# A hybrid encoder layer on one core: fp16 high and low parts for the dense products of its four passes, with scales from bounds that the chip computes

## The chip, the cores and the metric

The kernel runs on one core of one Trainium2 chip. The time is the device time of one execution in microseconds (us), and the figure for a kernel is the median of its runs. Before the change it is 2885.89 us (three runs, 2879.7 to 2888.39). The engines are called as in the profile: PE is TensorE, with PEld for its weight loads, DVE is VectorE, ACT is ScalarE, POOL is GpSimd, and SP is SyncE, whose queue issues the transfers (DMA).

## What is computed

One encoder layer on x of 2048 tokens by 1024 features and a memory of 256 tokens, all in float32. From the reference, cut to what matters:

```python
y = rmsnorm(h, norm_mix_g) @ w_in            # q, k, v (512 each), conv a and g (512 each)
att  = dilated_sliding_attention(q, k, v)     # three windows: (128,1), (512,4), (2048,16)
conv = conformer_conv(a, g, conv_w, conv_b, conv_ln_g, conv_ln_b)
h = h + concatenate([att, conv]) @ w_out      # 1024 x 1024
xq = rmsnorm(h, norm_x_g) @ w_xq              # 4 heads of 256
mn = rmsnorm(mem, norm_mem_g); xk, xv = mn @ w_xk, mn @ w_xv
pr = softmax(einsum('bshd,bmhd->bhsm', xq, xk) * 256 ** -0.5)
h = h + einsum('bhsm,bmhd->bshd', pr, xv) @ w_xo
u = rmsnorm(h, norm_mlp_g) @ w_up             # 1024 x 4096
h = h + square(relu(u)) @ w_down              # 4096 x 1024
return rmsnorm(h, norm_final_g)
```

## The kernel before

The matrices are worked in tiles of 128 by 128 weights against 512 columns (tokens). To keep float32's accuracy, each factor is split into a high and a low part, and each product is three matmuls, high by high, high by low and low by high (`mm3`, L248 to L252; the three matmuls are the lines L250, L251 and L252 of the profile).

The work has these stages, in order of time:

- **Memory, to about 140 us** (`memory`, L404). The memory's keys are folded with w_xq into the scratch array `ascr`, its values with w_xo into `bscr`. So cross attention becomes two dense products, with `ascr` (called xs) and with `bscr` (called x). Beside it `xprep` (L378) normalises x, turns it and splits it; the squares of its rows go through a tile "junk" (L366).
- **The w_in products, about 140 to 440 us.** Units `glu` (L566, tiles g00, a00, g10, a10), `lin_qk` (L670, tiles kr, qr, k0, q0, k1, q1, k2, q2) and `lin_v` (L623) run through `pipeline` (L550), which starts a unit's load, its scale and its split some steps ahead of its matmuls. Here the split is already fp16: `wscale` (L183) squares a raw weight tile on ACT with a sum (L189), and `pow2` (L168) makes a power of two from it by a small PE product (tile p, L173), a POOL power and DVE steps; `wsplit16` (L203) scales the tile (L207), casts its high part to fp16 on ACT and takes the low part on POOL. Parts of the convolution's sums (tile cacc, L267, on DVE) are woven in.
- **Far attention, to about 755 us**, with the rest of the `glu` units woven in. Outputs of attention and convolution go as high and low parts into the scratch arrays `cath` and `catl`.
- **Four passes of 512 tokens** (`post(p)`, L1310), from about 755 us to the end. Each does the product with w_out (called o), the product with ascr (xs), a softmax (tile xp), the product with bscr (x), then eight groups of w_up (up) and w_down (dn). The last pass has its own form of the MLP (`last_mlp`, L1459), where w_down is applied with seven products in place of eight on sums of halves.

In the passes each weight tile of 512 KB goes through `wpost` (L1179). SP loads it into one of two buffers "raw"; `wsplit2` makes the parts:

```python
    def wsplit2(wp, raw, name, bufs=2, shape=(P, 8, P), lo_eng=None):
        hi = wp.tile(list(shape), F32R, tag="whi", name=f"whi_{name}", bufs=bufs)
        lo = wp.tile(list(shape), F32R, tag="wlo", name=f"wlo_{name}", bufs=bufs)
        ACT.copy(hi, raw)                                               # L240
        (lo_eng or DVE).tensor_tensor(lo, raw, f(hi), op=ALU.subtract)  # L241
```

F32R is the form of float32 that PE takes at one pass. The split tiles alternate between two pools of two, so four are alive. A finished product is added to the residual stream h on DVE (L1303 for o and x, L1430 for dn, L1571 in the last MLP), and h is split again with a gain (L1304 on ACT, L1305 on DVE).

While pass p runs, two side streams are woven between its steps: the near attention of pass p+1 and its convolution. `weave` (L93) sets how many of their steps go with one step of the main stream. The order of the program is written by hand this way; a scheduler then orders each engine's queue by estimated times. Each engine takes its queue in order, and so does SP: a load that waits for its buffer holds back all loads behind it.

Of the kernel before, what the change touches and what calls it, by code (L numbers as in the profile page):

```python
# [48 lines left out]
def hybrid_layer(ctx, tc, A, out):  # L49
# [67 lines left out]
    cath = [dr.tile([P, S], F32R, name=f"cath{k}") for k in range(KC)]  # L117
    catl = [dr.tile([P, S], F32R, name=f"catl{k}") for k in range(KC)]
# [19 lines left out]
    cst.tile([P, 56], F32, name="cpad")  # L138
# [8 lines left out]
    def setup():  # L147
# [15 lines left out]
        sq = lp.tile([P, 8], F32, tag="nsq", name="gsq")  # L163
        ACT.activation(sq, gv[:, 0:8], AF.Square, accum_out=sx[:, 3:4])
        pow2(sx[:, 0:1], sx[:, 1:2], sx[:, 3:4], 1024.0)
        DVE.tensor_scalar(gmix, gv[:, 0:8], sx[:, 0:1], None, op0=ALU.mult)

    def pow2(mul, inv, ss, target, *names):  # L168

        with ExitStack() as st:  # L170
            after(st, *names)
            pc = ps("c", "p2")
            PE.matmul(pc[:, 0:1], onesq, ss, start=True, stop=True)  # L173
            v = lp.tile([P, 4], F32, tag="p2", name="p2", bufs=2)
            DVE.tensor_scalar(v[:, 0:1], pc[:, 0:1], 1e-30, None, op0=ALU.max)
            POOL.tensor_tensor(v[:, 1:2], v[:, 0:1], mhalf, op=ALU.pow)
            DVE.tensor_scalar(v[:, 2:3], v[:, 1:2], target, None, op0=ALU.mult)
            DVE.tensor_scalar(mul.bitcast(I32), v[:, 2:3].bitcast(I32), 0x7F800000, None, op0=ALU.bitwise_and)
            DVE.reciprocal(inv, mul)
# [3 lines left out]
    def wscale(raw, key):  # L183

        if key in tiles_scaled:
            return
        n = tiles_scaled[key] = 4 * len(tiles_scaled)
        q = lp.tile([P, 1024], BF16, tag="wjunk", name="wjunk")
        ACT.activation(q, raw.rearrange("p a b -> p (a b)"), AF.Square, accum_out=wsc[:, n + 3:n + 4])  # L189
        pow2(wsc[:, n:n + 1], wsc[:, n + 1:n + 2], wsc[:, n + 3:n + 4], 32768.0, "pe", "dve")  # L190
        t = wsc[:, n + 1:n + 2]
        DVE.tensor_tensor(t, t, sx[:, 1:2], op=ALU.mult)
        if key[0] == "a":
            c = cw[:, key[1]]
            DVE.tensor_scalar(c, c, t, None, op0=ALU.mult)
        else:
            DVE.tensor_scalar(wsc[:, n + 2:n + 3], t, 0.5 if key[0] == "g" else -0.125, None, op0=ALU.mult)
# [39 lines left out]
    def wsplit2(wp, raw, name, bufs=2, shape=(P, 8, P), lo_eng=None):  # L237
        hi = wp.tile(list(shape), F32R, tag="whi", name=f"whi_{name}", bufs=bufs)
        lo = wp.tile(list(shape), F32R, tag="wlo", name=f"wlo_{name}", bufs=bufs)
        ACT.copy(hi, raw)  # L240
        (lo_eng or DVE).tensor_tensor(lo, raw, f(hi), op=ALU.subtract)  # L241
# [31 lines left out]
    def conv_ln(n, alloc):  # L273
# [45 lines left out]
        for c in range(4):  # L319
            th_ = alloc("hi", F32R, f"lh{n}_{c}")  # L320
            tl_ = alloc("lo", F32R, f"ll{n}_{c}")
            ACT.copy(th_, cs[c])
            POOL.tensor_tensor(tl_, cs[c], f(th_), op=ALU.subtract)
            dma(f(cath[4 + c][:, sl]), f(th_))
            dma(f(catl[4 + c][:, sl]), f(tl_))
# [5 lines left out]
    xna = {n: pool(f"x{n}", stack=lin) for n in (2, 3)}  # L331
    lp = pool("lin", stack=lin)
    onesq = lp.tile([P, P], F32, name="onesq")
    DVE.memset(onesq, 1.0)
    gmix = lp.tile([P, 8], F32, name="gmix")
    sx = lp.tile([P, 4], F32, name="sx")
    wsc = lp.tile([P, 96], F32, name="wsc")
    lp.tile([P, 248], F32, name="lpad")
    xna.update({n: pool(f"x{n}", stack=early, side="right") for n in (0, 1)})
    XH_ = {}  # L340
# [5 lines left out]
    def xtiles(n):  # L346
        for i in range(KC // 2):
            for part, dst in (("h", XH_), ("l", XL_)):
                t = xpool(part, i, n, f"x{part}{i}_{n}", dtype=F16)
                dst[2 * i, n], dst[2 * i + 1, n] = t[:, 0], t[:, 1]  # L350
# [17 lines left out]
    def rstd_nat(sp, nat, name):  # L368
# [5 lines left out]
        DVE.tensor_tensor(ss[:, 0:n], ss[:, 0:n], ss[:, n:2 * n], op=ALU.add)  # L374
        rstd_col(r[:, 0:n], ss[:, 0:n], n, sp)
# [28 lines left out]
    def memory(sp):  # L404
# [76 lines left out]
        for h in range(XH):  # L481
            wt, wts = wts, []
            for k2 in range(4):
# [8 lines left out]
                DVE.tensor_tensor(ev, pt, rbm.rearrange("p q m -> p (q m)"), op=ALU.mult)  # L492
                dma(ascr[h // 2, :, 2 * k2:2 * k2 + 2, 256 * (h % 2):256 * (h % 2) + 256],
# [14 lines left out]
        for h in range(XH):  # L508
            wt, wts = wts, []
            for mc in range(2):  # L510
                for nh in range(2):
# [8 lines left out]
                    ACT.activation(ev, pt, AF.Copy, scale=rmem[:, mc:mc + 1])  # L520
                    dma(bscr[4 * nh:4 * nh + 4, :, 2 * h + mc, :].rearrange("m p c -> p m c"),
# [28 lines left out]
    def pipeline(*units):  # L550

        for _ in range(3):
            next(units[0])
        for _ in range(2 if len(units) > 1 else 0):
            next(units[1])
        for i, u in enumerate(units):
            if i + 1 < len(units):
                next(units[i + 1])
            if i + 2 < len(units):
                next(units[i + 2])  # L560
            for j, _ in enumerate(u):
                if j == 0 and i + 2 < len(units):
                    next(units[i + 2])
                yield

    def glu(c, ns, fine=False):  # L566
# [4 lines left out]
        def unit(x, c0):  # L571
# [3 lines left out]
            wscale(raw, (x, c))  # L575
# [47 lines left out]
    def lin_v(g, ns):  # L623
# [6 lines left out]
        yield  # L630
        wh = lbv.tile([P, 8, 256], F16, tag="wvh", name=f"wvh{g}{ns[0]}")
# [38 lines left out]
    def lin_qk(isq, c):  # L670
# [6 lines left out]
        if c == "r":  # L677
# [4 lines left out]
            wscale(raw, key)  # L682
# [5 lines left out]
        else:  # L688
# [3 lines left out]
            wscale(raw, key)  # L692
# [108 lines left out]
    with ExitStack() as st:  # L801
# [16 lines left out]
        drain(later)  # L818
    edges()
    vsc = vscale()  # L820
    with ExitStack() as st:
# [3 lines left out]
        weave(islice(steps, 31), (vsc, 0.42), (conv0, 0.58))  # L825
        drain(vsc, conv0)
        next(steps)
    with ExitStack() as st:
# [3 lines left out]
        for _ in range(4):  # L832
            next(steps)
        weave(islice(steps, 8), (conv0, 1))
        for _ in range(4):
            next(steps)
        weave(steps, (conv0, 2.2))
        drain(conv0)
# [136 lines left out]
    def combine(p, pr, o0):  # L975
# [46 lines left out]
        ct = [cats[0][x, pr] if end else aq.tile([P, 512], F32R, tag=f"ct{x}", name=f"ct{x}{p}{pr}") for x in "hl"]  # L1022
        with ExitStack() as st:
# [4 lines left out]
            vs = vinv[:, pr:pr + 1]  # L1028
            ACT.activation(ct[0], pt, AF.Copy, scale=vs)
            DVE.scalar_tensor_tensor(ct[1], pt, vs, f(ct[0]), op0=ALU.mult, op1=ALU.subtract)  # L1030
        for t, d in () if end else zip(ct, (cath, catl)):
            dma(f(d[pr][:, 512 * p:512 * (p + 1)]), f(t))
# [146 lines left out]
    def wpost(src, name, shape=(P, 8, P)):  # L1179
# [5 lines left out]
        return wsplit2(wq if n % 4 > 1 else wp, raw, name, shape=shape)  # L1185
# [3 lines left out]
    def ahead(m):  # L1189
# [4 lines left out]
        wout[m] = wsplit2(wp, raw, f"o0{m}")  # L1194
# [48 lines left out]
    def xquad(q, j, name):  # L1243
        return xp_.tile([P, 4, 512], F32R, tag=f"x{q}{j}", name=name)

    def ytile(q, k, name, dtype=F32R):
# [33 lines left out]
    def load_pair(p, half, j):  # L1280
        for q, src in (("h", cath), ("l", catl)):
            for e in range(1 if p == 0 and half and j else 2):
                k = 4 * (1 - half) + 2 * j + e
                dma(f(cats[p][q, k]), f(src[k][:, 512 * p:512 * (p + 1)]))

    def resid_linear(load, rhs, korder, resid, hs, ssum, key, y, name, steps=False, wide=False):


        for ms in ((0, 1, 2, 3) if wide else (0, 1, 2), () if wide else (3,), (4,), (5,), (6,), (7,)):
# [3 lines left out]
            for ks in [korder[a:b] for a, b in zip(cuts, cuts[1:])] if len(ms) > 1 else (korder,):  # L1293
                for m, (wh, wl) in zip(ms, wt):
# [6 lines left out]
                    if ks[-1] == korder[-1]:  # L1301
                        h = hs[m]
                        last["dve"] = DVE.tensor_tensor(h, pts[m], resid(m), op=ALU.add)  # L1303
                        ACT.activation(y["h", m], h, AF.Copy, scale=gain(key, m))  # L1304
                        DVE.scalar_tensor_tensor(y["l", m], h, gain(key, m), f(y["h", m]), op0=ALU.mult,  # L1305
                                                 op1=ALU.subtract)
# [3 lines left out]
    def post(p):  # L1310
# [9 lines left out]
        def from_x(m):  # L1320
# [6 lines left out]
        yield from resid_linear(lambda m: wout[m] if p == 0 and m in wout else wpost(wcols(w_out, m * P), f"o{p}{m}"),  # L1327
                                cats[p], [4, 5, 6, 7, 0, 1, 2, 3], from_x, hs, ssum, "x", y, f"o{p}_",
                                p == 0, p == 0)
        rs = rstd_from(ssum)  # L1330
# [356 lines left out]
```

## Time and profile before

| | before |
|---|---|
| median of the runs | 2885.89 us |
| the profiled execution | 2877.99 us, its span 2876.2 us |
| mean granted clock of PE | 0.988 |
| PE busy | 2783.7 us, 97% of the span |
| DVE busy | 1979.6 us, 69% |
| ACT busy | 1250.5 us, 43% |
| POOL busy | 467.2 us, 16% |
| moved by DMA | 434.27 MB, mean 151 GB/s |

The shares are means over stages that differ. A busy PE is not a PE at its peak, since a matmul's time in the records overlaps that of the next; the interval between the starts of two matmuls tells the rate.

### The profile page before, as it was taken

The page shows a single profiled execution, that of the slowest core. Times are in us where ns is not written, and L with a number is a line of the kernel's source. Part 1 is how long each engine was busy: PE and PEld are TensorE (multiplying, and loading weights), DVE is VectorE, ACT ScalarE, POOL GpSimd, SP SyncE. Part 2 cuts the span into 40 slices and gives each one's busy share as a digit, 9 for nine tenths or more (in the row PEclk, how much of TensorE's full clock was granted, in tenths as well). Part 3 has the DMA queues.
Part 4 walks back from the last instruction along what each step waited for, and adds up shares of the span by engine and source line. Part 5 has one row for each costly group of instructions (what it writes and reads, how often), then busy time and mean ns, then how long its engine had stood idle before and what let it go on. Part 6 is the DMA issues. An engine that isn't in the chain of part 4 may idle for free.

```text
span 2876.2 us, 41437 instructions
## 1 busy us (share of the span) xinstructions
PE 2783.7 (97%) x15474; PEld 2211.0 (77%) x15474; DVE 1979.6 (69%) x3579; ACT 1250.5 (43%) x2089; POOL 467.2 (16%) x500
## 2 busy tenths in 40 slices
PE   7889999988899999999999999999999999999998
PEld 7844467667688888888888888888888888888887
DVE  5636645555589886556887865579887556569886
ACT  5644332365454333434543334345433434444443
POOL 1236531121201111210020112001120110000000
PEclk9999999999999999999999999999999999999999
DMA  9968864789744544555444545544444445223342
GB/s 265 291 150 215 209 171 109 182 229 249 196 124 127 139 128 125 161 150 176 117 126 130 138 126 163 163 137 127 132 129 139 133 158 181 87 85 99 92 117 66
DMA packets 590729, 434.27 MB, mean 151 GB/s; under 512 B 191581, under 2 KB 508433, under 8 KB 590016
## 3 DMA queue, kind: packets, MB, share of 16 engines
q1 hardware_dynamic: 549776, 407.68, 50.4%
q10 hardware_dynamic: 38528, 17.93, 2.4%
q0 software_dynamic: 2224, 6.01, 0.6%
q8 instruction: 122, 2.00, 0.3%
q14 instruction: 79, 0.65, 0.1%
HBM read 340.42 MB, written 91.11 MB: 150 GB/s over the span
## 4 chain that ended last, share of the span: by engine, by line
PE 59%; DVE 5%; DMA 2%; ACT 1%; issue 1%; POOL 1%; SPq 0%; ACTq 0%; POOLq 0%; DVEq 0%
PE dn L250 7%; PE dn L252 7%; PE dn L251 7%; PE up L250 7%; PE up L252 7%; PE up L251 7%; DVE cacc L267 2%; PE o L251 2%; PE o L250 2%; PE o L252 2%; PE xs L250 2%; PE xs L252 2%; PE xs L251 1%; PE s L1082 1%; DMA cath<-lh 1%; PE pt L860 1%
## 5 line engine op out<-in xcount | busy, mean ns | idle before, releaser
L250 PE MATMUL up<-mh,whi_u 128*128 128x512 f32 x1024 | 403.4, 394 | 0.0
L251 PE MATMUL up<-ml,whi_u 128*128 128x512 f32 x1024 | 399.6, 390 | 2.4 <-DVE ml L1305 2.4
L252 PE MATMUL up<-mh,wlo_u 128*128 128x512 f32 x1024 | 399.2, 390 | 0.0
L267 DVE SCALAR_TENSOR_TENSOR cacc<-cu,cw,cacc 128x512 f32<-128x512 f32 x480 | 384.7, 802 | 5.1
L250 PE MATMUL dn<-hhh,whi_d 128*128 128x512 f32 x768 | 299.1, 399 | 1.1 <-ACT hhh L1416 1.1
L251 PE MATMUL dn<-hhl,whi_d 128*128 128x512 f32 x768 | 298.6, 391 | 0.6 <-DVE hhl L1417 0.6
L252 PE MATMUL dn<-hhh,wlo_d 128*128 128x512 f32 x768 | 298.2, 391 | 0.0
L240 ACT CAST whi_u<-raw_u 128x1024 fp32r<-128x1024 f32 x128 | 134.6, 1051 | 262.6 <-PE dn L251 187.9
L240 ACT CAST whi_d<-raw_d 128x1024 fp32r<-128x1024 f32 x100 | 105.1, 1051 | 317.1 <-PE up L251 270.9
L251 PEld LDWEIGHTS up<-ml,whi_u 128*128 128x128 f32 x1024 | 192.5, 188 | 41.2 <-DVE ml L1305 3.7
L252 PEld LDWEIGHTS up<-mh,wlo_u 128*128 128x128 f32 x1024 | 192.2, 188 | 40.5
L250 PEld LDWEIGHTS up<-mh,whi_u 128*128 128x128 f32 x1024 | 192.4, 188 | 37.3
L241 DVE TENSOR_TENSOR wlo_u<-raw_u,whi_u 128x1024 fp32r<-128x1024 f32 x128 | 160.8, 1257 | 45.7 <-ACT whi_u L240 40.5
L1430 DVE TENSOR_TENSOR h<-h,dn 128x512 f32<-128x512 f32 x192 | 128.5, 683 | 84.0 <-PE dn L252 83.1
L1414 DVE SCALAR_TENSOR_TENSOR rl<-up,ssumx 128x512 f32<-128x512 f32 x96 | 66.0, 690 | 167.3 <-PE up L252 166.5
L853 DVE CUSTOM_DVE_ANT_0 sm<-s,mask 128x256 f32<-128x256 f32 (+1 forms) x384 | 127.9, 374 | 69.5 <-PE s L1082 47.3
L252 PEld LDWEIGHTS dn<-hhh,wlo_d 128*128 128x128 f32 x768 | 144.1, 188 | 30.7
L250 PEld LDWEIGHTS dn<-hhh,whi_d 128*128 128x128 f32 x768 | 143.7, 188 | 29.7 <-ACT hhh L1416 1.3
L251 PEld LDWEIGHTS dn<-hhl,whi_d 128*128 128x128 f32 x768 | 144.6, 188 | 28.3 <-DVE hhl L1417 1.5
L864 DVE TENSOR_TENSOR pl<-pt,ph 128x512 f16<-128x512 f32 x160 | 109.8, 687 | 54.6 <-ACT ph L863 53.9
L227 POOL TENSOR_TENSOR nr<-st_v,mhalf 128x4 f32<-128x4 f32 (+1 forms) x15 | 14.3, 950 | 817.3 <-DVE st_v L223 817.3
L854 ACT ACTIVATE sm<-sm,o 128x256 f32<-128x256 f32 (+1 forms) x288 | 116.9, 454 | 59.4 <-DVE o L853 58.5
(497 smaller groups left out, 6945.9 us busy)
## 6 DMA issues: line engine op xcount, KB each, us to landing
raw_u<-in_w_up_dram SPq DMA_DIRECT2D x128, 512.0 KB
raw_d<-in_w_down_dram SPq DMA_DIRECT2D x100, 512.0 KB
raw_o<-in_w_out_dram SPq DMA_DIRECT2D x32, 512.0 KB
raw_a<-ascr SPq DMA_DIRECT2D x32, 512.0 KB
raw_b<-bscr SPq DMA_DIRECT2D x32, 512.0 KB
b<-in_w_down_dram SPq DMA_DIRECT2D x28, 512.0 KB
k<-kscr SPq DMA_DIRECT2D x24, 512.0 KB
k<-kscr SPq DMA_DIRECT2D x8, 1152.0 KB
```

The source lines that it names most:

```text
L240: ACT.copy(hi, raw)
L241: (lo_eng or DVE).tensor_tensor(lo, raw, f(hi), op=ALU.subtract)
L250: PE.matmul(o, lh, rh, start=first, stop=False, skip_group_check=more)
L251: PE.matmul(o, lh, rl, start=False, stop=False, skip_group_check=more)
L252: last["pe"] = PE.matmul(o, ll, rh, start=False, stop=end, skip_group_check=more)
L267: DVE.scalar_tensor_tensor(acc, u[:, t:t + 512], cw[:, c, t:t + 1], acc, op0=ALU.mult, op1=ALU.add)
L853: last["dve"] = DVE.tensor_tensor_reduce(dst, so, mask[:, 256 * m:256 * m + nk], 1.0, 3e38, ALU.add, ALU.min, mn)
L854: last["act"] = ACT.activation(dst, dst, AF.Exp, bias=mn, scale=-1.0)
L860: last["pe"] = PE.transpose(pt[:, j, :], sm[:, j, :], ident)
L864: DVE.tensor_tensor(pl, pt, ph, op=ALU.subtract)
L1414: last["dve"] = DVE.scalar_tensor_tensor(r, pt, 0.0, rsb, op0=ALU.max, op1=ALU.mult)
L1430: last["dve"] = DVE.tensor_tensor(hs[m], hs[m], pt, op=ALU.add)
```

## The change

**fp16 in the passes.** High and low parts of weights and activations of the five dense products become fp16 in place of F32R, and so do `cath` and `catl`, with half the bytes. fp16 has a small range, so every factor gets a power of two as scale, and the product is scaled back where it is used:

```diff
-        ACT.copy(hi, raw)
-        (lo_eng or DVE).tensor_tensor(lo, raw, f(hi), op=ALU.subtract)
+        ACT.activation(hi, raw, AF.Copy, scale=scale)
+        DVE.scalar_tensor_tensor(lo, raw, scale, hi, op0=ALU.mult, op1=ALU.subtract)
```

```diff
-                        last["dve"] = DVE.tensor_tensor(h, pts[m], resid(m), op=ALU.add)
-                        ACT.activation(y["h", m], h, AF.Copy, scale=gain(key, m))
+                        g = gains[:, m:m + 1]
+                        last["dve"] = DVE.scalar_tensor_tensor(h, pts[m], scale, resid(m), op0=ALU.mult, op1=ALU.add)
+                        ACT.activation(y["h", m], h, AF.Copy, scale=g)
...
-                    last["dve"] = DVE.tensor_tensor(hs[m], hs[m], pt, op=ALU.add)
+                    last["dve"] = DVE.scalar_tensor_tensor(hs[m], pt, K_DN, hs[m], op0=ALU.mult, op1=ALU.add)
```

The adds of `last_mlp` change in the same way. `conv_ln` gets one more POOL product per tile (16 in all), for the scale of its output.

**The scales.** They come from the sums of squares of the weights, so every weight has to be seen before its first use. New generators load the weights a first time and square them on ACT:

```diff
+    def scan(sc):
+        def one(src, shape, i):
+            t = sc.tile([P, 1024], F32, tag="scan", name=f"scan{i}", bufs=3)
+            q = sc.tile([P, 1024], BF16, tag="sjunk", name=f"sjunk{i}")
+            dma(t.rearrange("p (a b) -> p a b", a=shape), src)
+            yield
+            ACT.activation(q, t, AF.Square, accum_out=acc2[:, i:i + 1])
+        gens = [one(wcols(w_up, P * i), 8, i) for i in range(32)]
+        gens += [one(wcols(w_out, 0, 1024, rows=(i, i + 1)), 1, 32 + i) for i in range(8)]
+        yield from loads_ahead(gens)
...
+    def scan_down(sc):
+        def one(i):
+            t = sc.tile([P, 1024], F32, tag="scan", name=f"scand{i}", bufs=2)
+            q = sc.tile([P, 1024], BF16, tag="sjunk", name=f"sjunkd{i}")
+            dma(t, w_down[P * i:P * i + P, :])
+            yield
+            ACT.activation(q, t, AF.Square, accum_out=acc2[:, 76 + i:77 + i])
+        yield from loads_ahead([one(i) for i in range(32)])
...
+        pow2(S_DN, I_DN, None, 16384.0, "dve", of=t)
```

`loads_ahead` issues the load of a tile one step before the square of the one ahead of it. `scan` has 40 tiles of 512 KB, `scan_down` 32. In `memory`, each of the 32 tiles that go to `ascr` and `bscr` gets a square as well, through the tile "junk":

```diff
+                q_ = sp.tile([P, 512], BF16, tag="junk", name="junk", bufs=1)
+                ACT.activation(q_, ev, AF.Square, accum_out=acc2[:, 36 + 4 * h + k2 + 4:37 + 4 * h + k2 + 4])
```

`bounds` follows `scan`: one PE product that sums over the partitions, some 40 DVE operations on single columns, and four calls of `pow2` for the scales of weights and activations.

**Where this stands.** The scans are woven into the w_in products and into the first nine steps of pass 0:

```diff
+    scn = chain(scan(scp), bounds())
...
-        weave(islice(steps, 31), (vsc, 0.42), (conv0, 0.58))
+        weave(islice(steps, 31), (vsc, 0.42), (conv0, 0.58), (scn, 0.4))
...
-        weave(steps, (conv0, 2.2))
-        drain(conv0)
+        weave(islice(steps, 4), (scn, 1))
+        weave(islice(steps, 8), (conv0, 1), (scn, 1))
+        weave(islice(steps, 4), (scn, 1))
+        weave(steps, (conv0, 2.2), (scn, 2))
+        drain(conv0, scn)
...
+            dsc = scan_down(pp)
...
+        if p == 0:
+            weave(islice(main, 9), (dsc, 4), *sides)
+            drain(dsc)
```

**w_in's scales a step later.** `wscale` now yields between the square and `pow2`, and `pipeline` starts its first two units one step further ahead:

```diff
         ACT.activation(q, raw.rearrange("p a b -> p (a b)"), AF.Square, accum_out=wsc[:, n + 3:n + 4])
+        yield
         pow2(wsc[:, n:n + 1], wsc[:, n + 1:n + 2], wsc[:, n + 3:n + 4], 32768.0, "pe", "dve")
...
-        for _ in range(3):
+        for _ in range(4):
             next(units[0])
-        for _ in range(2 if len(units) > 1 else 0):
+        for _ in range(3 if len(units) > 1 else 0):
             next(units[1])
```

Some small constants move to another pool, and the tiles of x for token groups 2 and 3 are laid out anew, so that the scan's buffers find room where group 2's pool lay.

258 lines of the change are left out of this document (185 added, 73 removed).

## The prediction

> **What bounds the kernel now.** The first view is the page's table of engines: TensorE (PE) is busy for nearly the whole span and no other engine for more than 69%. I read next the windows view, because a mean over 2.9 ms says nothing about a stage.
>
> ```profile
> span 2876.2 us, 41437 instructions
> PE 2783.7 (97%) x15474; PEld 2211.0 (77%) x15474; DVE 1979.6 (69%) x3579; ACT 1250.5 (43%) x2089; POOL 467.2 (16%) x500
> DVE  5636645555589886556887865579887556569886
> ```
>
> ```profile
> 70.00:110.00 40.00, 37.24 (x316) 36.99 (x315) 33.98 (x54) 25.08 (x47) 13.31 (x10) 1.00 1.05 332
> 140.00:200.00 60.00, 51.17 (x244) 25.63 (x245) 24.64 (x57) 31.65 (x47) 21.64 (x18) 0.94 0.53 125
> 180.00:190.00 10.00, 7.69 (x33) 3.74 (x32) 2.89 (x9) 6.58 (x11) 3.32 (x3) 0.83 0.66 175
> 200.00:260.00 60.00, 53.70 (x256) 25.85 (x254) 30.75 (x48) 31.91 (x41) 36.33 (x35) 0.94 0.84 217
> 260.00:330.00 70.00, 65.88 (x304) 30.12 (x303) 54.22 (x81) 25.67 (x33) 41.37 (x40) 0.98 0.94 214
> 735.00:755.00 20.00, 9.13 (x49) 6.69 (x50) 3.20 (x11) 2.49 (x7) 1.44 (x2) 0.66 0.94 258
> 755.00:865.00 110.00, 107.61 (x607) 89.41 (x607) 88.82 (x180) 54.47 (x104) 12.55 (x14) 1.00 0.49 137
> 864.00:936.00 72.00, 71.13 (x411) 58.74 (x410) 66.64 (x121) 36.23 (x60) 11.96 (x13) 1.00 0.45 126
> ```
>
> The columns are the window, then busy us of PE, weight loads, VectorE (DVE), ScalarE (ACT) and GpSimd (POOL), the granted clock, the DMA share and GB/s. Three regimes stand there. From 755 us on, in the four passes, PE is the bound, but in the densest window DVE has 66.6 of 72 us filled. From 140 to 330 us, where the w_in products run, PE has 19 us of idle time in 190 and the DMA engines are already at 0.53, 0.84 and 0.94. Around 735–755 PE waits for transfers, and its granted clock is 0.66. The change makes the first regime's instructions shorter, and puts its extra work into the second and into the beginning of the first.
>
> **The gain on PE.** The groups of instructions give the counts, the timeline the interval between two matmuls that follow each other (a single one's duration overlaps its neighbours).
>
> ```profile
> L250 PE MATMUL up<-mh,whi_u 128*128 128x512 f32 x1024 | 403.4, 394 | 0.0
> L250 PE MATMUL dn<-hhh,whi_d 128*128 128x512 f32 x768 | 299.1, 399 | 1.1 <-ACT hhh L1416 1.1
> L250 PE MATMUL o<-cath,whi_o 128*128 128x512 f32 x256 | 102.5, 402 | 2.1 <-DMA cath<-cath 1.4 <-ACT cath L1029 0.7
> L250 PE MATMUL xs<-whi_a,yh 128*128 128x512 f32 x256 | 101.4, 398 | 0.0
> L250 PE MATMUL x<-pth,whi_b 128*128 128x512 f32 x256 | 100.7, 399 | 0.7 <-ACT pth L1357 0.7
> L250 PE MATMUL dn<-whi_d,hqh 128*128 128x512 f32 x112 | 43.7, 390 | 0.5 <-ACT hqh L1482 0.5
> L250 PE MATMUL dn<-whi_d,hz 128*128 128x512 f32 x84 | 32.7, 389 | 0.0
> L250 PE MATMUL dn<-whi_d,hhh 128*128 128x512 f32 x32 | 12.3, 389 | 0.0
> ```
>
> ```profile
> 2000.00 0.39 PE L252 MATMUL x<-pth,wlo_b 128*128 128x512 f32 x1
> ...
> 2002.72 0.39 PE L252 MATMUL x<-pth,wlo_b 128*128 128x512 f32 x1
> ```
>
> ```profile
> 299.54 0.38 PE L251 MATMUL lin<-xl,whi_k 128*128 128x512 f16 x1
> ...
> 302.99 0.38 PE L252 MATMUL lin<-xh,wlo_k 128*128 128x512 f16 x1
> ```
>
> Each group has two equal partners, L251 and L252, so the matmuls that change are 3 x (1024 + 768 + 256 + 256 + 256 + 112 + 84 + 32) = 8364. In the fp32r run 12 intervals take 2.72 us, 226.7 ns each; in the fp16 run of the w_in products, which is the same three-product form, 16 take 3.45 us, 215.6 ns. That is 11.1 ns x 8364 = 92.8 us. PE is the bound there, so it is a gain: **-93**.
>
> **What DVE and ACT pay.** The residual adds and the lower halves of the weights become scaled operations.
>
> ```profile
> L241 DVE TENSOR_TENSOR wlo_u<-raw_u,whi_u 128x1024 fp32r<-128x1024 f32 x128 | 160.8, 1257 | 45.7 <-ACT whi_u L240 40.5 <-DMA catl<-ll 4.9
> L1430 DVE TENSOR_TENSOR h<-h,dn 128x512 f32<-128x512 f32 x192 | 128.5, 683 | 84.0 <-PE dn L252 83.1
> L1305 DVE SCALAR_TENSOR_TENSOR yl<-h,gv,yh 128x512 fp32r<-128x512 f32 x32 | 23.4, 747 | 0.0
> L240 ACT CAST whi_u<-raw_u 128x1024 fp32r<-128x1024 f32 x128 | 134.6, 1051 | 262.6 <-PE dn L251 187.9 <-DMA raw_u<-in_w_up_dram 31.1 <-PE dn L252 17.5
> L207 ACT ACTIVATE raw_a<-raw_a,wsc 128x1024 f32<-128x1024 f32 x8 | 9.2, 1145 | 23.6 <-DMA raw_a<-in_w_in_dram 20.9 <-DVE wsc L178 2.7
> ```
>
> An operation on two tensors with a column scalar takes 747 ns, the plain one 683: +64 ns. By the program's loops there are 88 weight tiles and 80 residual adds in each of three passes and 109 and 122 in the last: 735 x 64 ns = 47 us of DVE over the 2010 us from 865 to the end; if the extra doubles with the 1024-wide tile, 71 us. ACT's scaled copy takes 1145 against 1051 ns, 373 x 94 ns = 35 us, on an engine that has half of its time free (36 of 72 us in the dense window): nothing. For DVE, the 72 us of the dense window shrink to 68.6 us on PE (5% of it, 11.1/226.7) while DVE's 66.6 grow by its share of 47 us, 72 x 47/2010 = 1.7, to 68.3 us. [...] The page's row of DVE has three slices of 40 at 9 tenths and ten at 8; each slice is 72 us and would gain 3.4. I let the three lose all of it, and the ten about a tenth of a slice's gain: 10 + 4, **+14**, with ends 5 and 44 (all thirteen slices gain nothing).
>
> **The scans in the w_in stage.** Forty new loads of 512 KB, each squared by ACT, go before the end of the w_in products; their results are needed by the first split of w_out, which is much later, so nothing waits for the values. What waits is what is queued behind: SP issues in order, and a scan load with three buffers waits until ACT has squared the load three back. In the changed program's issue order, 17 of the loads stand ahead of raw_kr, and they stand between raw_g10, raw_a10 and the late x rows; ten more stand ahead of raw_k0, three ahead of raw_q0. On ACT, the casts of w_in stand behind the squares. The 32 new squares of the memory stage share one buffer with the squares of x, which pushes the preparation of the later x tiles back.
>
> ```profile
> 145.46 0.37 SPq L58 DMA_DIRECT2D raw_g<-in_w_in_dram  x1
> ```
>
> ```profile
> 149.24 1.06 ACT L189 ACTIVATE wjunk<-raw_g 128x1024 bf16<-128x1024 f32 x1 [5.06 <-DMA raw_g<-in_w_in_dram]
> 150.20 0.19 ACT L189 ACTIVATION_READ_ACCUMULATOR wjunk<-raw_g 128x1 f32 x1
> ```
>
> ```profile
> PE p L173 <- ACT wjunk L189: 8.0, 3, 5.4
> ```
>
> A load takes 3.78 us from issue to ACT's square, and the square with its read 1.25: with three buffers one scan per (3.78 + 1.25)/3 = 1.68 us, 67 us for 40. By bytes: the stage 70–110 moved 332 GB/s at a full share, so 512 KB are 1.58 us and 40 of them 63 us. Free capacity from 140 to 330 us is 0.47 x 60 + 0.16 x 60 + 0.06 x 70 = 42 us. So some 21 us do not fit, if the stage is DMA-bound to its end; the late x tiles and the casts behind squares cost more at the beginning, and the third row shows that PE waits here for just this kind of chain (8.0 us for three squares of raw tiles). The later hand-out of the scales by a step takes about those 8 us away. I set 21 + 15 - 8 = **+28**, ends 10 (the loads fill the gaps) and 67 (none is hidden).
>
> A sentence that the sum can do without: the Trainium skill, DMA: Bandwidth & Descriptors, "Anatomy of one DMA — SWDGE (gpsimd) path", gives about 2.0 us fixed and bytes/436 GB/s per transfer, 3.2 us for 512 KB, for loads issued by GpSimd. The row above has 3.78 for one issued by SP; by the page's figure a scan would be (3.2 + 1.25)/3 = 1.5 us and the whole 60 us at most, estimated.
>
> **The scan of w_down in pass 0.** Thirty-two more loads and squares, with two buffers, between the first steps of pass 0 and ahead of raw_b02 on SP.
>
> ```profile
> 792.70 0.34 SPq L58 DMA_DIRECT2D raw_a<-ascr  x1
> 826.86 0.32 SPq L58 DMA_DIRECT2D raw_b<-bscr  x1
> ```
>
> ```profile
> 796.83 1.05 ACT L240 CAST whi_a<-raw_a 128x1024 fp32r<-128x1024 f32 x1 [2.14 <-DMA raw_a<-ascr]
> ```
>
> A load of this stage takes 4.13 us to its user; (4.13 + 1.25)/2 = 2.69 us per scan, 86 us for 32. By bytes they fit: 32 x 1.58 = 51 us in the free 0.51 x 110 = 56. But the chain is serial. If it starts at 755, thirty scans have passed at 755 + 30 x 2.69 = 836 us, and the first tile of bscr, issued at 826.86 now, comes 9 us later; a square that waits behind casts, and transfers that share with the scans, add some more: **+15**, ends 3 and 45 (half of the chain bare).
>
> **The rest.** The scratch copies of the concatenation halve:
>
> ```profile
> PE o L251 <- DMA catl<-catl: 7.7, 2, 6.2
> ```
>
> About half of that wait goes, -4. The chain of bounds (some 45 short DVE steps and five round trips through POOL), and 16 more POOL products in the convolution's norm, stand beside busy PE: +1. Idle time costs clock: in 180–190, 2.31 us of idle go with a clock of 0.83, 1.7 us lost, most of it inside the idle itself; for 43 us of new waits I add 5. **+2** in all, ends -4 and +10.
>
> **Sum**: -93 + 14 + 28 + 15 + 2 = -34. The profiled execution took 2877.99 us (span 2876.2); it becomes 2844. The median shown, 2885.89, is 7.9 above it, so the predicted median is **2852 us**.
>
> **Rivals.**
>
> *The scans are not hidden* (0.22). In-order queues make the scans a serial chain: 67 + 86 = 153 us bare. The balance without them is -93 + 14 + 2 = -77, so the kernel gets slower once more than 77 us of the 153, half, are bare. With 110 bare (the first chain whole, half of the second) it is -77 + 110 = +33: 2919 us. For it: 0.94 of the DMA is used already at 260–330, and both chains stand ahead of PE's own weights. Against: ACT and DMA have free time from 140 to 200 and from 755 to 865.
>
> *DVE sets the pace of the passes* (0.13). The thirteen dense slices gain nothing, 13 x 3.4 = 44 in place of 14: 2882 us, or a few less. For it: 68.3 against 68.6. Against: ten of these slices have 8 tenths and room.
>
> *The clock falls in the waits* (0.07). In 735–755 PE is idle for 10.87 us and loses 0.34 x 20 = 6.8 us of clock, 0.63 per us of idle; at that price 43 us of waits cost 27 in place of 5: 2874 us. The Trainium skill, TensorE: Matmul & The Clock Gate, "HAM oscillation — how this bites in real kernels", says that waits for DMA longer than a window of about 3.4 us put PE at half clock until it has been busy again. The low clocks of the two rows agree, where waits are long.
>
> *Nearly all is hidden* (0.10). With 10 + 3 for the scans: -64, 2822 us.
>
> *fp16 gives no shorter interval in the passes* (0.03), because DVE and attention matmuls between them break the run: gain 0, +59, 2945 us. The run at 299.54 speaks against it.
>
> The forecast itself, scans that cost 25 to 60 us, has 0.45: 2834 to 2869.
>
> **How the numbers follow.** A measurement of this kernel tells about 0.3% from no change, 8.7 us: faster means under 2877, slower over 2894.5. Faster: 0.43 of the forecast's 0.45, 0.06 of DVE's 0.13, 0.10, and 0.06 of the clock's, 0.65. The same: 0.02, 0.07, 0.01, and 0.02 of the scans that lie near the edge, 0.12. Slower: 0.20 and 0.03, 0.23. The range goes from 2812 (all hidden, DVE costs its lower end) to 2930 (some 120 us of scans bare); beyond are about 0.05 and 0.10.
>
> **What would show it.** In the profile after, consecutive products of the passes should start every 215.6 ns, and a window around 864–936 have DVE at 68 of 69 us. The beginning of kr, q1 and of pass 0 against before show the first scan's price: pass 0 some 25 us later. From there to the softmax's second product the w_down scans cost 15, and PE's waits name whi_b. If pass 0 starts over 60 us later, or the stage after it is 40 longer, the scans rule and the forecast is wrong; if both are right and the end is late, it is DVE: its idle time before the weight splits gone, and PE waiting for wlo.

## The result

The changed kernel takes 2858.8 us (2856.15 to 2859.55, four runs) against 2883.03 for the kernel before on the same chip: a ratio of 0.9913, 95% interval 0.9893 to 0.9932. The forecast was 2852, range 2812 to 2930, faster. The profiled execution took 2859.55 us with a span of 2857.8.

The page of the changed kernel, its table of engines and its row of DVE by slices:

```profile
span 2857.8 us, 41763 instructions
PE 2702.5 (95%) x15482; PEld 1486.6 (52%) x15482; DVE 2017.9 (71%) x3647; ACT 1379.2 (48%) x2295; POOL 489.6 (17%) x521
DVE  6534664565567798756799886679979655579997
```

PE is busy for 81 us less, in a span that is only 18 us shorter: PE now has idle time which it did not have. DVE grew by 38 us, ACT by 129. The windows view of the changed kernel (columns as before: window; busy us of PE, weight loads, DVE, ACT and POOL; granted clock, DMA share, GB/s) says where the idle time is:

```profile
180.00:190.00 10.00, 6.20 (x25) 3.72 (x25) 7.18 (x17) 10.00 (x20) 6.71 (x6) 0.56 1.07 323
200.00:260.00 60.00, 49.90 (x224) 24.33 (x223) 26.78 (x40) 40.33 (x57) 19.84 (x20) 0.89 1.04 262
260.00:330.00 70.00, 48.54 (x215) 21.59 (x213) 37.14 (x61) 36.79 (x55) 36.60 (x35) 0.85 1.04 268
755.00:865.00 110.00, 93.49 (x592) 54.20 (x592) 66.75 (x158) 63.19 (x118) 18.12 (x26) 0.89 0.86 246
864.00:936.00 72.00, 54.83 (x280) 29.56 (x279) 48.70 (x107) 43.86 (x90) 4.32 (x5) 0.83 0.60 185
1944.00:2016.00 72.00, 72.00 (x446) 39.85 (x443) 64.83 (x132) 41.34 (x84) 5.47 (x5) 1.00 0.45 125
2664.00:2736.00 72.00, 72.00 (x335) 32.69 (x334) 69.26 (x98) 35.61 (x47) 0.00 (x0) 1.00 0.34 104
```

The early stage has the DMA engines full (1.04) and PE idle for 32 of 130 us; the beginning of pass 0 has PE idle for 34 of 181. The later passes have PE full. The interval, from the timeline of the changed kernel in pass 2:

```profile
2005.12 0.38 PE L393 MATMUL x<-ptl,whi_b 128*128 128x512 f16 x1
...
2007.28 0.38 PE L394 MATMUL x<-pth,wlo_b 128*128 128x512 f16 x1
```

Ten intervals in 2.16 us, 216 ns each. The scaled operations, from the groups of instructions:

```profile
L382 ACT ACTIVATE whi_u<-raw_u,bd 128x1024 f16<-128x1024 f32 x128 | 146.8, 1147 | 257.3 <-PE dn L393 163.8
L383 DVE SCALAR_TENSOR_TENSOR wlo_u<-raw_u,bd,whi_u 128x1024 f16<-128x1024 f32 x128 | 169.5, 1324 | 33.8 <-ACT whi_u L382 33.6
L1586 DVE SCALAR_TENSOR_TENSOR h<-dn,bd,h 128x512 f32<-128x512 f32 x192 | 140.4, 745 | 72.8 <-PE dn L394 72.7
```

From the two timelines one can read when PE begins each part of the work (us from the start of the span, one profiled execution each; the last row is the last down product). The columns beside the first two are kernels of the experiments below.

| first product of | before | after | no first scan | no w_down scan | neither scan | neither, 4-byte parts |
|---|---|---|---|---|---|---|
| tile q0 of w_in | 273.4 | 314.6 | 281.7 | 312.8 | 282.1 | 281.8 |
| pass 0 (o) | 738.1 | 779.1 | 749.8 | 779.0 | 755.1 | 757.6 |
| up, pass 0 | 911.0 | 976.7 | 945.0 | 951.1 | 925.7 | 936.9 |
| pass 1 | 1302.6 | 1357.7 | 1324.7 | 1330.5 | 1306.8 | 1335.2 |
| pass 2 | 1848.7 | 1879.2 | 1846.9 | 1852.0 | 1832.5 | 1886.7 |
| pass 3 | 2392.1 | 2395.9 | 2365.2 | 2371.2 | 2351.7 | 2435.4 |
| last down | 2867.6 | 2848.6 | 2817.8 | 2823.9 | 2805.2 | 2916.7 |

The changed kernel is 41 us behind at the start of pass 0, 66 behind at its first up product, and gains 85 from there on. A few us in this table say little: the kernels without the first scan and without both do the same work up to pass 0, and begin it at 749.8 and 755.1.

### The profile page after: what moved, and what is told of

Same layout as the page of the kernel before. It is cut to its first block, busy times and chain, and to the rows that moved or that the text cites. A ratio compares the mean times of both kernels' runs of the same rounds, so it can differ in the third digit from the quotient of the medians.

```text
span 2857.8 us, 41763 instructions
## 1 busy us (share of the span) xinstructions
PE 2702.5 (95%) x15482; PEld 1486.6 (52%) x15482; DVE 2017.9 (71%) x3647; ACT 1379.2 (48%) x2295; POOL 489.6 (17%) x521
## 4 chain that ended last, share of the span: by engine, by line
PE 48%; DVE 3%; issue 2%; DMA 2%; POOL 1%; ACT 0%; SPq 0%; POOLq 0%; DVEq 0%; ACTq 0%
PE dn L392 6%; PE dn L394 6%; PE dn L393 6%; PE up L392 6%; PE up L393 6%; PE up L394 6%; PE o L392 1%; PE o L394 1%; PE o L393 1%; PE xs L392 1%; PE xs L394 1%; PE xs L393 1%; PE s L1236 1%; PE pt L1014 1%; DVE cacc L409 1%
## 5 line engine op out<-in xcount | busy, mean ns | idle before, releaser
L392 PE MATMUL up<-mh,whi_u 128*128 128x512 f16 x1024 | 389.4, 381 | 7.5 <-ACT mh L1460 3.8
L393 PE MATMUL up<-ml,whi_u 128*128 128x512 f16 x1024 | 389.1, 380 | 1.2 <-DVE ml L1461 1.2
L394 PE MATMUL up<-mh,wlo_u 128*128 128x512 f16 x1024 | 387.9, 380 | 0.0
L394 PE MATMUL dn<-hhh,wlo_d 128*128 128x512 f16 x768 | 291.3, 380 | 0.0
L393 PE MATMUL dn<-hhl,whi_d 128*128 128x512 f16 x768 | 290.8, 380 | 0.0
L392 PE MATMUL dn<-hhh,whi_d 128*128 128x512 f16 x768 | 283.8, 380 | 0.1
L382 ACT ACTIVATE whi_u<-raw_u,bd 128x1024 f16<-128x1024 f32 x128 | 146.8, 1147 | 257.3 <-PE dn L393 163.8
L383 DVE SCALAR_TENSOR_TENSOR wlo_u<-raw_u,bd,whi_u 128x1024 f16<-128x1024 f32 x128 | 169.5, 1324 | 33.8 <-ACT whi_u L382 33.6
L1586 DVE SCALAR_TENSOR_TENSOR h<-dn,bd,h 128x512 f32<-128x512 f32 x192 | 140.4, 745 | 72.8 <-PE dn L394 72.7
L393 PEld LDWEIGHTS <-whi_u 128*128 128x128 f16 x1024 | 100.7, 98 | 119.0 <-issue 6.3
L392 PEld LDWEIGHTS <-whi_u 128*128 128x128 f16 x1024 | 100.8, 99 | 116.2 <-issue 2.7
L383 DVE SCALAR_TENSOR_TENSOR wlo_d<-raw_d,bd,whi_d 128x1024 f16<-128x1024 f32 x100 | 132.9, 1329 | 23.1 <-ACT whi_d L382 22.8
```

The source lines that it names most:

```text
L382: ACT.activation(hi, raw, AF.Copy, scale=scale)
L383: DVE.scalar_tensor_tensor(lo, raw, scale, hi, op0=ALU.mult, op1=ALU.subtract)
L392: PE.matmul(o, lh, rh, start=first, stop=False, skip_group_check=more)
L393: PE.matmul(o, lh, rl, start=False, stop=False, skip_group_check=more)
L394: last["pe"] = PE.matmul(o, ll, rh, start=False, stop=end, skip_group_check=more)
L1586: last["dve"] = DVE.scalar_tensor_tensor(hs[m], pt, K_DN, hs[m], op0=ALU.mult, op1=ALU.add)
```

## The experiments

The kernel before, run beside each of them on the same chip, had medians of 2881 to 2884 us; the ratios are to those.

**Each scan left out, and both.** The loads and squares go, and constants take the place of the sums:

```diff
-        yield from loads_ahead(gens)                                 # in scan
+        DVE.memset(acc2[:, 0:40], 1.0)
...
-        yield from loads_ahead([one(i) for i in range(32)])          # in scan_down
+        DVE.memset(acc2[:, 76:108], 0.25)
```

> Leaves out the forty loads and squares of w_up and w_out; constants stand in the place of their sums of squares. Theory M (milestones): pass 0 starts 41 us later than before because of this scan, and nearly all of it comes back: 2820 us, 39 below the changed kernel's 2859. Rival R (the rest of the early stage): the later x tiles, the memory's new squares and the scales a step later make half of the delay: about 2838. By the prediction's term of 28 it would be 2831.

Measured 2827.57 us, ratio 0.981 (0.9793 to 0.9827): 31 us come back, between theory M's 39 and rival R's 21, and near the prediction's 28.

> Leaves out the 32 loads and squares of w_down in pass 0; constants stand for their sums. Theory M: from the start of pass 0 to its first up product before takes 172.9 us and the changed kernel 197.6, though fp16 should have shortened the stretch by some 25 us; so this scan costs about 50 us: 2809 us. Rival P (the prediction's term): it costs 15 and the stretch is slow for another reason, scaled operations on DVE or the side streams: 2844.

Measured 2834.4, ratio 0.9828 (0.9814 to 0.9843): 24 come back, nearer to rival P's 15 than to theory M's 50. The 50 rested on a count that was wrong: from the start of pass 0 to its first up product there are 576 products that change, not some 2300, so fp16 could shorten that stretch by 6 us and not by 25. Without the scan it takes 172.1 us, before 172.9: the 6 are not seen either.

> Leaves out both scans. Theory M: the two costs add up, 2859 - 39 - 50 = 2770 us, which is 113 under before; more than the 93 of the shorter matmuls, since the scratch halves and the passes give some more. Rival P: 2859 - 28 - 15 = 2816, the passes limited by DVE for the rest.

Measured 2808.07, ratio 0.9734 (0.9717 to 0.9751): 51 come back, a little less than 31 + 24, so the prices nearly add. Theory M's 2770 is refuted; rival P's 2816 is 8 off. (The profiled execution of this kernel took 2816.22, 8 above its median; the table's column is that one's.) So the change is worth -75 without the scans, and the scans take 51 of it.

**Transfers or squares.** One kernel keeps all loads and squares 8 columns of each tile; the other keeps all squares, on a tile that is filled once, and has no loads.

```diff
-            ACT.activation(q, t, AF.Square, accum_out=acc2[:, i:i + 1])
+            ACT.activation(q[:, 0:8], t[:, 0:8], AF.Square, accum_out=bd[:, 60:61])   # loads only
...
-            dma(t.rearrange("p (a b) -> p a b", a=shape), src)                        # squares only
```

> Keeps the 72 loads of both scans and squares only 8 columns of each tile; constants stand for the sums. The scans together cost 51 us (2859 against 2808 without both). Theory D (the transfers are the price: the DMA share is 1.04 at 140 to 330 us): at most 8 come back, 2851 to 2859. Theory S (the squares in ACT's queue are the price): most come back, about 2815.

Measured 2855.72, ratio 0.9909 (0.9887 to 0.9932).

> Keeps the 72 full squares on ACT, on a tile filled once, and leaves out the loads of both scans. Theory D: near the kernel without scans, 2808 to 2816. Theory S: most of the 51 us stay, about 2850. If both this and the one with loads alone are fast, it is the chain of the two through few buffers that costs.

Measured 2840.46, ratio 0.9856 (0.9834 to 0.9879). Against the 2808 without scans the loads alone cost 48, the squares alone 32, both together 51. Neither theory holds as it was put: the loads alone reach nearly the whole price, and the squares alone over half of it. That the second adds little because it runs in time that PE has already lost is a reading, and was not shown. And the loads alone are not the transfers alone: the short squares still stand in ACT's queue, where between 200 and 330 us seven of them wait 10.4 us in all for their loads. Windows 200 to 330 and 780 to 865 us, of the kernels with loads only, with squares only, and with neither:

```profile
200.00:330.00 130.00, 94.06 (x399) 43.53 (x400) 63.96 (x105) 58.04 (x109) 58.42 (x56) 0.82 1.04 269
780.00:865.00 85.00, 70.11 (x383) 36.34 (x384) 49.73 (x100) 35.62 (x88) 10.93 (x13) 0.89 0.92 284
```

```profile
200.00:330.00 130.00, 102.47 (x470) 48.59 (x468) 71.00 (x106) 72.10 (x102) 64.19 (x59) 0.89 0.76 180
780.00:865.00 85.00, 73.16 (x405) 37.95 (x403) 53.98 (x101) 65.47 (x112) 9.81 (x11) 0.91 0.56 162
```

```profile
200.00:330.00 130.00, 119.44 (x545) 55.56 (x543) 82.96 (x128) 60.08 (x73) 75.07 (x70) 0.93 0.84 203
780.00:865.00 85.00, 82.58 (x479) 43.63 (x477) 69.37 (x134) 40.90 (x70) 7.92 (x10) 1.00 0.45 133
```

With loads only, the DMA share goes from 0.84 to 1.04 and PE loses 25 of 130 us. With squares only the share falls to 0.76 and PE still loses 17: ACT is busy for 72 us of 130, far from full, but its queue is in order. PE's waits between 140 and 330 us in the changed kernel name one result above all (total us, times, longest), and ACT's timeline shows what it stood behind (the short reads of the sums left out):

```profile
PE lin L392 <- ACT whi_q L351: 11.2, 1, 11.2
```

```profile
303.65 6.72 ACTq L58 DMA_DIRECT2D kscr<-sth_k  x3
310.42 1.06 ACT L225 ACTIVATE sjunk<-scan 128x1024 bf16<-128x1024 f32 x1 [7.66 <-DMA kscr<-sth_k]
...
311.48 1.13 ACT L349 ACTIVATE raw_q<-raw_q,wsc 128x1024 f32<-128x1024 f32 x1
312.52 1.04 ACT L225 ACTIVATE sjunk<-scan 128x1024 bf16<-128x1024 f32 x1
...
313.55 1.03 ACT L351 CAST whi_q<-raw_q 128x1024 f16<-128x1024 f32 x1
```

ACT's idle time of 7.66 us is not a square's wait for its load: the loads in flight had been issued by 297.42 us and had landed by 303.05. ACT itself issues three writes of sth_k here (`ACTq`, which does not count as busy), and they hold its queue for 1.86, 1.66 and 3.12 us, while the DMA share is 1.12. With loads only they take 2.36, 2.60 and 2.11 us at a share of 1.18. Without the first scan they take 0.33, 0.54 and 0.32 at 0.88, and with squares only 0.33, 0.54 and 1.61 at 0.56. So the extra loads reach PE at this place through the engine that casts its weights, because that engine also issues transfers; why an issue takes longer when the share is full is not shown. The two squares add 2.1 us, and without the first scan the same wait of PE is 1.5 us.

In pass 0 a square does wait for its load, and the cast ph of the attention stands behind it (ACT, then PE):

```profile
818.20 1.06 ACT L247 ACTIVATE sjunkd<-scand 128x1024 bf16<-128x1024 f32 x1 [2.83 <-DMA scand<-in_w_down_dram]
819.17 0.18 ACT L247 ACTIVATION_READ_ACCUMULATOR sjunkd<-scand 128x1 f32 x1
819.26 0.57 ACT L1017 CAST ph<-pt 128x512 f16<-128x512 f32 x1
```

```profile
819.88 0.20 PE L1022 MATMUL opt<-v,ph 128*128 128x65 f16 x1 [3.02 <-ACT ph L1017]
```

From the start of pass 0 to its first up product (779 to 977 us), PE waits 9.8 us for ph in the changed kernel, and 0.7 us over the same stretch of the kernel without this scan:

```profile
PE opt L1022 <- ACT ph L1017: 9.8, 4, 3.4
```

**Who issues the loads.**

```diff
-            dma(t, w_down[P * i:P * i + P, :])
+            dma(t, w_down[P * i:P * i + P, :], nc.scalar)      # in scan too
```

> The whole computation; both scans' loads are issued by ACT in place of SP, nothing else moves. Theory Q (the price is SP's queue in order: loads of w_in and w_out stand behind a scan load that waits for its buffer): 25 us or more come back, under 2835. Theory B (the price is the transfers' share of the DMA engines, whoever issues them): 2850 to 2860.

Measured 2884.49, ratio 1.0006 (0.9991 to 1.0021): 26 us worse than the changed kernel, outside both expectations. Pass 0 starts at 802 us in place of 779. So ACT, whose queue already delays PE, is a worse place for the issues. It does not clear SP's queue: what the loads cost there and what they cost on ACT changed together.

**What fp16 alone is worth.** All parts get their 4-byte form back; scales and scaled adds stay, both scans stay out.

```diff
-        hi = wp.tile(list(shape), F16, tag="whi", name=f"whi_{name}", bufs=bufs)
+        hi = wp.tile(list(shape), F32R, tag="whi", name=f"whi_{name}", bufs=bufs)
```

> Leaves out both scans as in the kernel of 2808 us, and gives the parts of the dense products their old 4-byte form back, with all scales and scaled adds kept. Theory G (fp16 is worth its 93 us and DVE takes 14 of them): under the slower matmuls DVE's additions are covered, so 2808 + 79 + 4 for the scratch halves = 2891. Theory N (DVE takes nothing, the missing 13 lie elsewhere): 2808 + 93 + 4 = 2905.

Measured 2923.68, ratio 1.0141 (1.0113 to 1.0169). fp16 is worth 116 us (2924 - 2808, the halved scratch included), more than the 93 of either theory; and without it the rest of the change, scans aside, costs 41. From the start of pass 0 to the last down product this kernel takes 2159 us and the kernel before 2130, with the same matmuls. PE is full in both:

```profile
L393 PE MATMUL up<-mh,whi_u 128*128 128x512 f32 x1024 | 405.7, 396 | 1.2 <-ACT mh L1461 1.2
```

So it is mostly the interval. Over all pairs of neighbouring products in the passes it is 227.4 to 228.4 ns before (by kind of product, pauses over 0.3 us left out), 230.2 to 231.0 in this kernel, and 215.8 to 215.9 in the changed kernel. Over all kinds the mean is 227.8 before and 230.5 here, and the 2.7 ns are 23 us over 8364 products. Pauses of about 0.32 us between two 4-byte products, 2 to 5% of the pairs, are there in both kernels with 4-byte parts; in the changed kernel they are at most 0.1%. What it has instead are 60 pairs at 0.40 to 0.45 us, 57 of them at a granted clock of 0.5. With all pauses the mean of up is 230.2 before and 217.3 after.

**Are the longer weight splits the cause?** The same kernel with the plain copy and subtraction:

```diff
-        ACT.activation(hi, raw, AF.Copy, scale=scale)
-        DVE.scalar_tensor_tensor(lo, raw, scale, f(hi), op0=ALU.mult, op1=ALU.subtract)
+        ACT.copy(hi, raw)
+        DVE.tensor_tensor(lo, raw, f(hi), op=ALU.subtract)
```

> As the kernel of 2924 us (4-byte parts, no scans), with the weights split by the plain copy and subtraction of before, so without their scales; the residual adds and activations keep theirs. That kernel's passes took 30 us more than before's, with the same matmuls, their interval 230.9 against 228 ns. Theory V (the longer weight splits on DVE and ACT are the cause): 20 us or more come back, about 2900. Theory A (the residual adds or the altered order): 2915 to 2924.

Measured 2917.94, ratio 1.0118 (1.0097 to 1.0138): 6 us come back, which the two ratios' intervals do not tell from none, and the interval between products stays (230.2 to 231.0 ns). So the splits are not the cause of the 30 us; whether it is the scaled residual adds, the altered order of the queues or the tiles' places in memory was not tried.

**The memory's squares.** Without the scans pass 0 still starts 12 to 17 us late (749.8 and 755.1). The 32 squares of the memory stage left out:

```diff
-                ACT.activation(q_, ev, AF.Square, accum_out=acc2[:, 36 + 4 * h + k2 + 4:37 + 4 * h + k2 + 4])
```

> Leaves out both scans and the 32 squares of the memory stage too; constants stand for the sums. Without the scans pass 0 still starts 12 to 17 us later than before. Theory L (the squares share the one tile with the squares of x, and make the x tiles late): some 10 come back, 2798. Theory W (the later scales of w_in do it): 2806 to 2808.

Measured 2801.51, ratio 0.9724 (0.97 to 0.9748): 6.6 us less than without the scans by the medians, but the intervals of the two ratios overlap. Tile kr begins at 202.8 us in place of 210.0; pass 0 begins at 747.9, still 10 us after before. So it is theory L at most, with less than it claimed, and most of the late start stays open. The later hand-out of w_in's scales was not tried by itself.

**Places for the scans.** First the scan of w_down over twice the steps:

```diff
-            weave(islice(main, 9), (dsc, 4), *sides)
+            weave(islice(main, 18), (dsc, 2), *sides)
```

> The whole computation; only the scan of w_down is spread over 18 steps of pass 0 at rate 2 in place of 9 at rate 4, so that its loads reach into a stage with a DMA share of 0.46. Theory D (transfers and their place in SP's queue are the price): at least half of the 24 us of this scan come back, 2847 or less. Theory C (a fixed chain of load, square, buffer is the price wherever it stands): no change, 2859.

Measured 2848.57, ratio 0.9884 (0.9863 to 0.9906): 10 us better than the changed kernel by the medians, less than the half that theory D wanted. But the loads are not spread: SP issues the 32 from 789.0 to 895.5 us, in the changed kernel from 793.7 to 903.2, and the last square falls behind 343 of the 576 products of this stretch, there behind 366. From pass 0 to its first up product it takes 186.5 us in place of 197.6; why is not shown, and the scan's place was not tested. Then also the first scan out of the weave of the first w_in stage:

```diff
-        weave(islice(steps, 31), (vsc, 0.42), (conv0, 0.58), (scn, 0.4))
+        weave(islice(steps, 31), (vsc, 0.42), (conv0, 0.58))
```

> The whole computation; w_down's scan spread as in the other kernel, and the first scan left out of the stage from 200 to 330 us (DMA share 1.04 with it) and put into the stage of the last w_in products alone (0.64 before). Theory D: 15 to 25 of the first scan's 31 us come back too, about 2825. Theory C: 2859, or slower, since the bounds are ready later and w_out's first split waits for them.

Measured 2841.03, ratio 0.9858 (0.9835 to 0.9882). But tile q0 still begins at 312 us: in SP's queue the first scan's loads stand where they stood, since the scheduler pulls a load forward when its buffer is free, whatever the order it is written in (the last kernel bears this out). So this kernel did not test the first scan's place either, and the intervals do not tell its 8 us over the one before from none. To move the loads their buffers must come free later; the last kernel takes them from a pool that opens with the last w_in products:

```diff
-    scp = pool("scan", stack=early, side="right")
...
+        scn = chain(scan(pool("scan", stack=st)), bounds())      # in the block of lin_v
...
-                q_ = sp.tile([P, 512], BF16, tag="junk", name="junk", bufs=1)
+                q_ = sp.tile([P, 512], BF16, tag="junk2", name="junk", bufs=1)
```

> The whole computation. w_down's scan is spread as in the kernel of 2848.6 us; the first scan gets its buffers from a pool that opens with the last w_in products only, so that its loads really stand behind raw_v01 in SP's queue (in the kernel where only the weaving was moved they stood at the same places as before); and the memory's squares get a tile of their own. Theory D (the scan is cheap where the DMA engines are free): up to k2 the milestones are those of the kernel without scans (k2 at about 342 us in place of 380), some 10 us are paid later, the squares' own tile brings 5: 2820 us. Theory C (the price goes with the scan): k2 early, but pass 0 as late as in the changed kernel, 779 us, and 2843.

Measured 2840.39, ratio 0.9845 (0.9827 to 0.9863). Tile k2 begins at 347.1 us in place of 379.8, as without the scan; pass 0 begins at 774.6. The price went along: between 450 and 600 us, first the changed kernel, then this one:

```profile
450.00:600.00 150.00, 147.38 (x1116) 108.92 (x1114) 82.68 (x218) 45.87 (x88) 26.48 (x44) 0.99 0.46 125
```

```profile
450.00:600.00 150.00, 129.99 (x932) 89.75 (x931) 81.51 (x221) 71.15 (x139) 26.55 (x38) 0.93 0.79 215
```

The DMA engines have room here (0.79), and PE has 17 us more of idle time all the same; its waits in this stretch name ACT's cast whi_a (6.8 us) and the DVE steps of the bounds (5.4 and 5.2). That is theory C for the first scan; w_down's loads are no more spread here (788.4 to 896.8 us). This and the kernel before it are the fastest that keep the whole computation, 40 and 42 us under before; their intervals lie below that of the changed kernel.

## Why the prediction was right, and where not

**The balance** was right: -77 without the scans, -75 measured; +43 for the scans, 51 measured; faster, by 24 where 34 was forecast. That -77 and -75 agree is luck: the gain on PE was put 23 us too small, and the rest of the change, 14 + 2, some 25 too cheap (41 by the kernel with 4-byte parts).

**The gain on PE, -93**, was too small: 116 by the kernel with 4-byte parts. The working took an undisturbed run of 12 intervals, 226.7 ns, for the mean of the stage. The mean over the passes is 227.8 before and 215.9 in the changed kernel, 100 us over 8364 products; with pauses up to 1.5 us it is 230 to 235 before, by kind of product. The 116 are the price by this order of leaving out, from a kernel whose interval is 230.5. The sum had no term for the pauses or for an interval that other work lengthens. The rival that fp16 brings nothing is refuted by the same run.

**DVE, +14**, failed in its place and its mechanism: no run shows that the dense slices lose their gain. The single durations came as forecast: 745 ns against 683 for an add, 1324 against 1257 for a split, 1147 against 1051 on ACT, and 38 us more of DVE against 47. But 2664 to 2736 has DVE at 69.26 of 72 us and PE at 72.00, and the last pass went from 475.5 to 452.7 us, 22.8 where 2028 products give 22.5 at 11.1 ns and 24 by the means over all pairs. DVE at 96% did not hold PE back: from pass 1 to the end PE waits 6.5 us for DVE, before 2.5. What the rest of the change costs in the passes shows in the 4-byte kernel, 30 us, through the interval, and not as a wait for DVE. In fp16 the interval does not move, so whether those 30 are a price in the changed kernel at all cannot be read from it. The rival that DVE sets the pace is refuted.

**The first scan, +28.** Measured 31 for the scan alone, and 12 to 17 more for the late start that stays without it, of which the memory's squares are at most a part. The term had 21 for the loads, 15 for late tiles and casts, and took 8 off for the scales a step later. The -8 is the part that is not seen as time: PE's wait for the squares of raw tiles is gone from the list, but the same small products p wait 7.5 us for rbs, and casts that stand behind other work on ACT cost 11.2 and 5.8 us. That the DMA engines fill up was right (1.04). That this also lengthens ACT's own issues, and that the squares of the two scans cost 32 us without any load, was not foreseen.

**The scan of w_down, +15.** Measured 24, within its ends of 3 and 45, but by another wait. The chain did not start at 755 us but at 793.72, since pass 0 began 41 us later (it had begun at 738.1), and its last load was issued at 903.2: 3.5 us from load to load in place of 2.69. The working had it end at the weights of bscr, but PE's waits do not name whi_b; they name ph, 9.8 us, which stood behind the squares on ACT. SP's waits from 780 to 900 us show the chain, load for square and square for load:

```profile
SPq L58 <- ACT sjunkd L247: 32.9, 24, 2.6
SPq L58 <- DMA scand<-in_w_down_dram: 24.3, 16, 4.2
```

**The clock.** The rival gave 0.63 us per us of idle time. The mean granted clock fell from 0.988 to 0.972: 0.028 x 2858 = 80 us of clock against 0.012 x 2876 = 35 before. It stands at 0.5 for 160 us of the changed kernel and for 71 us before, and PE is busy for 99 and 48 of them. If PE does half as much in that time, 25 us more are lost while PE works; that is an estimate, near the rival's 27 and far from the forecast's 5. Without the scans PE is busy for 78 us at this clock, so about 15 of the 25 stay without them. These us are contained in the prices above, and were not tried apart from the waits.

```profile
175.00:185.00 10.00, 4.72 (x20) 3.40 (x18) 8.29 (x22) 9.12 (x17) 5.54 (x6) 0.50 1.06 303
```

The Trainium skill, TensorE: Matmul & The Clock Gate, "HAM oscillation — how this bites in real kernels", says that waits for transfers of over about 3.4 us halve the clock for a time. Here a wait of 3.52 us, for ACT's rbs and not for a transfer, ends at 173.68, ahead of the window shown; that agrees. But in the kernel before no wait of PE from 147 to 190 us is over 2.31 us, and the clock stands at 0.5 from 184.2 to 187.6 all the same. So the 0.83 that the prediction counted for the page does not come from a wait of that length.

**What would show it**, by the prediction's own list: the interval of 215.6 ns came; pass 0 began 41 us later, between the 25 forecast and the 60 that would have refuted it; the end was not late by DVE. Two signs did not come: 864 to 936 us has DVE at 48.70 of 72, since the dense stage came later and PE waited in it, and PE's waits do not name whi_b.

## What to carry to other kernels

A price for extra loads and squares can't be read from how much an engine or the DMA is idle on the mean: on queues in order, one square that waits for its load holds up the cast behind it, and either half of the pair is enough to make PE wait. An engine's idle time can also be its own issuing of transfers, so one looks at the issues on its queue before one calls it a wait. An interval between matmuls has to be taken over a whole stage, pauses included, and not over a clean run. Where a scheduler orders the queues, a written order need not move a load: here it moved neither scan's, and a pool that opened later moved one. One looks in the queue whether a load moved before one reads a time as a test of its place.

## What was not expected of the hardware

Products of 4-byte parts took 226.7 ns at best, 228 on the mean before and 231 in a kernel with the same matmuls and other work beside them; those of fp16 took 215.8 to 216.0 ns in every kernel here (pauses over 0.3 us left out). The weight load is the row in which they differ most, 188 ns of every 4-byte product and 98 of an fp16 one (groups, before and in the changed kernel):

```profile
L250 PEld LDWEIGHTS up<-mh,whi_u 128*128 128x128 f32 x1024 | 192.4, 188 | 37.3
L393 PEld LDWEIGHTS <-whi_u 128*128 128x128 f16 x1024 | 100.7, 98 | 119.0 <-issue 6.3
```

That the longer load is why the interval follows the other engines was not shown.
